# A hybrid decoder block on one core: memory attention by rounded parts, and elementwise work moved between VectorE and GpSimd

## The chip, the cores and the metric

The kernel runs on one core of a Trainium2 chip. The metric is the device time of one execution in microseconds (us). The engines are named as the profile names them: PE (TensorE matmuls), PEld (its weight loads), DVE (VectorE), ACT (ScalarE), POOL (GpSimd) and SP (SyncE, which here only issues DMAs). L12 is line 12 of the kernel before.

## The reference

One layer of a block with three mixers on 1024 tokens of width 1024, all in float32. Cut to what matters here:

```python
def hybrid_layer(x, mem, ...):
    h = rmsnorm(x, norm_g)
    proj = h @ w_in               # 1024 x 11280: the inputs of all branches and gates
    ...                           # gated DeltaNet branch, stick-breaking attention branch
    mkv = rmsnorm(mem, mem_norm_g) @ w_mem_kv      # 256 memory tokens
    mk, mv = jnp.split(mkv, 2, axis=-1)
    o_m = memory_attention(to_heads(m_q, 4), to_heads(mk, 4), to_heads(mv, 4))
    o_m = merge_heads(o_m) * jax.nn.silu(m_z)
    merged = g_dn * (o_dn @ w_br_dn) + g_sb * (o_sb @ w_br_sb) + g_m * (o_m @ w_br_mem)
    return x + merged @ w_out     # then a final rmsnorm

def memory_attention(q, mk, mv):  # 4 heads of 64
    s = jnp.einsum('bhtd,bhmd->bhtm', q, mk) * (1.0 / math.sqrt(q.shape[-1]))
    p = jax.nn.softmax(s, axis=-1)
    return jnp.einsum('bhtm,bhmd->bhtd', p, mv)
```

## The kernel before

**Products by rounded parts.** Most matmuls use the type fp32r. An operand is split into a high part (ACT copies it to fp32r) and a low part (DVE subtracts the high part from the source); `split` at L139 does both, and `mm3` at L153 multiplies as high x high + high x low + low x high. Products that stay in plain F32, the memory attention's among them, take a single call.

**The norm stage** (about the first 80 us). Rows of x are loaded 128 at a time into four buffers. `norm` (L270) squares on ACT, computes rs = 1/sqrt on POOL, and multiplies by the gain and rs: on DVE in one fused operation for the first two rows and the memory rows, or, with `on=gp`, as a product with the gain on POOL (L280) and a scaling on ACT (L284) for the other six rows of x. `two_rows` (L331) takes rows tb and tb+4, transposes them on PE, splits them into blocks A11, A12, A21, A22 and forms the sums S1 to S4 for a block scheme of Strassen and Winograd's kind, which saves one of eight block products in the large projection. The low parts of S1 to S4 are DVE subtracts of two SBUF tiles; those of the blocks read PSUM. Two row blocks at a time, `first_values` computes some values and the gates' inputs `bat`; its low part `svl` has one buffer, and POOL issues its store `sv_dl`. Beside this, `memory_kv` projects the memory tokens and stores mk and mv in DRAM (`kv_d`).

**The dense stream.** `stream` (L167) yields slots. One slot is one block product: 12 fp32r matmuls of 512 columns. A job has seven slots (B11, B21, T1, T2, T3, B22, T4) and four evacuations called `evac(i, j, a, b)`, the first of them, (0, 0), just before T2. Weights come over SP's queue into six buffers `wb`. All later stages call `slot()` between pieces of their own work, so the dense stream runs beside them.

**The decay tables.** After three slots the gate's chain on DVE (some 17 operations of 64 columns, ending in `gg`) feeds two small matmuls `gps` (L905), from which the tables come. They are stored and read back per head as `gam`; `decay` (L449) masks it on POOL and exponentiates it on ACT, at the first evacuation of each `kq_head`.

**The memory attention.** The job mq leaves q in SBUF (`mqT`), and `memory` (L659) is a generator whose steps are spread over 32 slots. Per head (64 channels) and per pair of token blocks: two score matmuls into a PSUM tile of the pair `wk`, the maximum on DVE, exponentials and scaling on ACT, four transposes on PE, a copy to `pT`. After four pairs come the values: two halves of two matmuls, a copy and a store. `combine` (the last part of the DeltaNet's triangular solve) uses the same two `wk` tiles in turn with it. The solver, a long chain on DVE, ends shortly after the memory attention starts.

**The order of the work.** The program is written in one order, and a scheduler orders each engine's instructions when the kernel is built. On the chip each engine and each DMA queue works through its list strictly in order. Tiles wait for the release of the buffer that they reuse.

Of the kernel before, what the change touches and what calls it, by code (L numbers as in the profile page):

```python
# [21 lines left out]
NT = 8  # L22
# [14 lines left out]
def hybrid_block(ctx, tc, x, mem, norm_g, mem_norm_g, wq, wv0, wba, convw, a_log, dt_bias,  # L37
# [51 lines left out]
    gp.memset(ones, 1.0)  # L89
    mhalf = cst.tile([P, 64], F32, name="mhalf")  # L90
    gp.memset(mhalf, -0.5)
# [31 lines left out]
    zm_d = dscr("zm_d", [2, P, T])  # L123
    kv_d = dscr("kv_d", [2, P, 2, 256])
    g_d = dscr("g_d", [3, 8, P, T])
# [12 lines left out]

    def split(dst, src):  # L139
        sc.activation(dst[0], src, AF.Copy)  # L140
        ve.tensor_tensor(out=dst[1], in0=src, in1=f(dst[0]), op=ALU.subtract)  # L141

# [117 lines left out]
    vp_ = pool("V0", 1, stack=v_st, side="right")  # L260
    bat = ap_.tile([P, NT, 16], F32, name="bat")

# [6 lines left out]

    def norm(xt, g_bc, nm, on=ve):  # L270

        sq = ap_.tile([P, T], mybir.dt.bfloat16, tag="sq", name="sq_" + nm)
        ss = ap_.tile([P, 1], F32, tag="ss", bufs=4, name="ss_" + nm)
        sc.activation(sq, xt, AF.Square, accum_out=ss)
        rs = ap_.tile([P, 1], F32, tag="rs", bufs=4, name="rs_" + nm)
        n = T // len(g_bc)
        halves = [(xt[:, j * n:j * n + n], g) for j, g in enumerate(g_bc)]
        if on is gp:
            for t, g in halves:
                gp.tensor_tensor(out=t, in0=t, in1=g, op=ALU.mult)  # L280
        gp.tensor_scalar(out=rs, in0=ss, scalar1=1.0 / T, scalar2=EPS, op0=ALU.mult, op1=ALU.add)
        gp.tensor_tensor(out=rs, in0=rs, in1=mhalf[:, 0:1], op=ALU.pow)
        if on is gp:
            sc.activation(xt, xt, AF.Copy, scale=rs)  # L284
        else:
            for t, g in halves:
                ve.scalar_tensor_tensor(out=t, in0=t, scalar=rs, in1=g, op0=ALU.mult, op1=ALU.mult)

    def transposed(xn, nm):
# [7 lines left out]
        return res  # L297

    def memory_kv():
        kv = [st.tile([P, 2, 256], F32, tag="st", bufs=3, name=f"kv{j}") for j in range(2)]  # L300
        for b in range(2):
            for q, ov in enumerate(transposed(mem_rows[b], f"m{b}")):
                split([t[:, q * 4:q * 4 + 4, b * P:b * P + P] for t in mHL], ov)
        for i in range(2):
            us = [unit(f"mk{i}_{j}", raw_unit(f"mk{i}_{j}", wmk[i, j])) for j in range(2)]
            o = psum("Y", f"mk_{i}")
            mm3(o[:, 0:256], [(us[k // 4][0][:, k % 4 * P:k % 4 * P + P], us[k // 4][1][:, k % 4 * P:k % 4 * P + P],
                               mHL[0][:, k, :], mHL[1][:, k, :]) for k in range(KC)])
            sc.activation(kv[0][:, i, :], o[:, 0:256], AF.Copy)
# [7 lines left out]
        sc.activation(kv[1], o.rearrange("p (a b) -> p a b", a=2), AF.Copy)  # L317
        for j in range(2):
            sc.dma_start(out=kv_d[j], in_=kv[j])

# [63 lines left out]
    for tb in range(1, 4):  # L384
        for b in (tb, tb + 4):
            if b not in rows_:
                rows_[b] = row(x, b)
            norm(rows_[b], [g1], f"x{b}", gp)
        two_rows(tb)()
# [53 lines left out]
    def kq_head(h):  # L443
# [68 lines left out]
        def evac(i, j, a, b):  # L512
            if (i, j) == (0, 0):
                decay()
            if j not in xps:
                xps[j] = xpad(cp, f"{'kq'[j]}{h}")
            put(xps[j][:, 4 + i * 512:516 + i * 512], a, b)
            if (i, j) == (0, 0):
                conv(0, 0)
            elif (i, j) == (0, 1):  # L520
                conv(1, 0)
                chunks(0)
                conv(1, 1)
            elif (i, j) == (1, 0):
                conv(0, 1)
                chunks(1)
                rows()
# [43 lines left out]
    def twice_silu(t, src, nm):  # L571

        th = mp_.tile([P, 512], F32, tag="th", bufs=2, name="th_" + nm)
        sc.activation(th, src, AF.Tanh, scale=0.5)
# [6 lines left out]

    mq = {}
# [76 lines left out]
    def memory():  # L659
        mkT, mv = (mp_.tile([P, 2, 256], F32, name=f"mkv{j}") for j in range(2))  # L660
        for j, t in enumerate((mkT, mv)):
            sy.dma_start(out=t, in_=kv_d[j])
        for h in range(4):
            r0 = (h % 2) * 64
            pT = mp_.tile([P, 2, T], F32, tag="pT", name=f"pT_{h}")
            for tb in range(0, NT, 2):
                s = psum("wk", f"ms_{h}_{tb}")
                for j in range(2):
                    pe.matmul(s[:, j * 256:(j + 1) * 256], mq[h // 2][r0:r0 + 64, (tb + j) * P:(tb + j + 1) * P],
                              mkT[r0:r0 + 64, h // 2, :], start=True, stop=True)  # L670
                sv = s.rearrange("p (a b) -> p a b", a=2)
# [15 lines left out]
                sc.activation(pT[:, :, tb * P:(tb + 2) * P], o.rearrange("p (a b) -> p a b", a=2), AF.Copy)  # L687
                yield
            for hf in range(2):
                mo = psum("wk", f"mo_{h}_{hf}")  # L690
                for c in range(2):
                    pe.matmul(mo[r0:r0 + 64, :], mv[:, c, h * 64:h * 64 + 64],
                              pT[:, c, half(hf)], start=(c == 0), stop=(c == 1))
                t = mp_.tile([P, 512], F32, tag="mot", bufs=1, name=f"mot_{h}_{hf}")
                sc.activation(t[r0:r0 + 64], mo[r0:r0 + 64], AF.Copy, scale=0.5)
                sc.dma_start(out=om_d[h // 2, r0:r0 + 64, half(hf)], in_=t[r0:r0 + 64])
            yield

# [103 lines left out]

    SOLVE, MEM, COMB, RECUR = 1 + 1 + 62 + 8, 4 * 5, 16, 1 + 16 * 4

# [56 lines left out]

    open_psum("psC", tr=2, wk=2, X=1)

    b_st = sub()
# [17 lines left out]

    aa, ab, ex, den, zz, z2, hr, sp, gg = (bt(n) for n in ("aa", "ab", "ex", "den", "zz", "z2", "hr", "sp", "gg"))
    ve.tensor_tensor(out=hn(aa), in0=bat[:, :, 8:16], in1=dtb.unsqueeze(1).to_broadcast([P, NT, H]), op=ALU.add)
# [8 lines left out]
    for c in (15, 13, 11, 9, 7, 5, 3):  # L893
# [5 lines left out]
                            op0=ALU.mult, op1=ALU.mult)  # L899
    for _ in range(3):  # L900
        slot()
# [19 lines left out]
    b_st.close()  # L921
    a_st.close()

    c_st = sub()
    cp = pool("C", 1, stack=c_st)
    until("kq7")
# [348 lines left out]
```

## Time and profile before

| | |
|---|---|
| median of 3 runs (lowest to highest) | 1628.33 us (1626.48 to 1635.07) |
| the profiled execution: time, span | 1628.7 us, 1627.0 us |
| its mean granted PE clock | 0.985 |
| busy share of the span: PE, PEld, DVE, ACT, POOL | 95%, 80%, 73%, 50%, 19% |
| DMA | 217.81 MB, mean 134 GB/s |

The span is the time from the first to the last instruction of the profiled execution. Busy shares are averages over the whole span; the stages differ, so the prediction reads them by stretches. "Idle before, releaser" in a row is the time for which the engine stood before the instruction, and what ended it.

### The profile page before, as it was taken

The numbers are of one execution on the slowest core, as the hardware profiler recorded it, in microseconds if no ns is written. First come the engines' busy times: TensorE is split into PE (matmuls) and PEld (weight loads), VectorE is DVE, ScalarE is ACT, GpSimd is POOL, SyncE is SP. The second block draws the span as 40 slices with busy tenths as digits, with TensorE's granted clock in tenths as the row PEclk, the third lists the DMA queues.
The fourth block names the chain that finished last, engine by engine and source line by source line (L and its number), as shares of the span: only waits on it lengthen the run. The fifth ranks groups of instructions, "written<-read, shape, count | busy, mean of one in ns | idle before, by whom it ended". The sixth has DMA issues, their size and how long they took to land.

```text
span 1627.0 us, 23179 instructions
## 1 busy us (share of the span) xinstructions
PE 1552.1 (95%) x7963; PEld 1294.8 (80%) x7963; DVE 1179.9 (73%) x1891; ACT 817.6 (50%) x1909; POOL 303.5 (19%) x557
## 2 busy tenths in 40 slices
PE   5889999999999999999999999999998899989998
PEld 4868888887888777776688888888886788878786
DVE  8869889888999998554588778777867554554333
ACT  7548778775555334555555555555544222232121
POOL 4314444351122110000011112111111111010011
PEclk8999999999999999999999999999998999999999
DMA  7236555564333445333222322332148765634232
GB/s 268 94 90 176 159 183 166 158 193 148 97 107 108 141 136 165 91 111 96 90 85 85 110 93 82 104 92 79 65 155 262 254 202 181 206 122 138 82 104 78
DMA packets 149063, 217.81 MB, mean 134 GB/s; under 512 B 39504, under 2 KB 66384, under 8 KB 148688
## 3 DMA queue, kind: packets, MB, share of 16 engines
q1 hardware_dynamic: 105824, 157.06, 32.2%
q10 hardware_dynamic: 34016, 29.89, 5.5%
q0 software_dynamic: 9104, 29.37, 4.8%
q8 instruction: 63, 1.03, 0.3%
q14 instruction: 56, 0.46, 0.1%
HBM read 147.48 MB, written 68.78 MB: 133 GB/s over the span
## 4 chain that ended last, share of the span: by engine, by line
PE 64%; DVE 4%; DMA 4%; issue 3%; ACT 1%; POOL 1%; SPq 0%; DVEq 0%; POOLq 0%; ACTq 0%
PE mmY_g L157 3%; PE mmY_g L159 3%; PE mmY_g L158 3%; PE mmY_skq L157 2%; PE aTp L1014 2%; PE mmY_skq L159 2%; PE mmY_skq L158 2%; PE out L1183 2%; PE out L1181 2%; PE out L1182 2%; PE y_ysb L1116 2%; PE y_ysb L1117 2%; PE y_ydn L1116 2%; PE y_ysb L1118 2%; PE y_ydn L1117 2%
## 5 line engine op out<-in xcount | busy, mean ns | idle before, releaser
L988 DVE TENSOR_TENSOR_SCAN pf<-pf 128x512 f32<-128x512 f32 (+4 forms) x96 | 97.2, 1013 | 16.4 <-POOL pf L986 16.4
L140 ACT ACTIVATE aTh<-aTp 128x512 fp32r<-128x512 f32 (+2 forms) x96 | 44.7, 498 | 62.2 <-PE aTp L1014 58.6
L973 POOL MEMSET pf<- 128x1 f32 x64 | 6.0, 98 | 342.7 <-PE aTp L1014 175.4
L141 DVE TENSOR_TENSOR aTl<-aTp,aTh 128x512 fp32r<-128x512 f32 (+2 forms) x96 | 50.4, 547 | 22.8 <-ACT aTh L140 22.6
L982 ACT ACTIVATE pf<-z 128x512 f32<-128x512 f32 (+4 forms) x96 | 47.1, 498 | 26.7 <-PE z L159 23.4
L986 POOL TENSOR_SCALAR_AFFINE_SELECT pf<-pf 128x128 f32<-128x128 f32 x64 | 24.9, 390 | 181.4 <-ACT pf L982 181.4
L991 DVE TENSOR_TENSOR pf<-be,pf 128x512 f32<-128x512 f32 (+4 forms) x96 | 53.7, 559 | 3.9
L647 DVE TENSOR_TENSOR M<-M,tmp 128x62 f32<-128x62 f32 (+30 forms) x62 | 53.6, 864 | 0.3
L644 DVE TENSOR_TENSOR tmp<-M 128x62 f32<-128x62 f32 (+30 forms) x62 | 53.3, 860 | 0.3
L1116 PE MATMUL y_ysb<-oh_sb,w_ysb 128*128 128x512 f32 x128 | 51.0, 399 | 2.0 <-ACT w_ysb L140 2.0
L1181 PE MATMUL out<-oh_wo,mh 128*128 128x512 f32 x128 | 50.0, 391 | 1.5 <-ACT mh L140 1.5
L1116 PE MATMUL y_ydn<-odnh,w_ydn 128*128 128x512 f32 x128 | 49.5, 391 | 1.8 <-ACT odnh L140 1.8
L1117 PE MATMUL y_ysb<-ol_sb,w_ysb 128*128 128x512 f32 x128 | 50.8, 397 | 0.0
L1118 PE MATMUL y_ysb<-oh_sb,w_ysb 128*128 128x512 f32 x128 | 50.8, 398 | 0.0
L1030 PE MATMUL av<-aTl,vh 128*128 128x256 f32 (+1 forms) x160 | 46.9, 293 | 3.4 <-DVE aTl L141 3.4
L1117 PE MATMUL y_ydn<-odnl,w_ydn 128*128 128x512 f32 x128 | 49.9, 390 | 0.0
L1118 PE MATMUL y_ydn<-odnh,w_ydn 128*128 128x512 f32 x128 | 49.9, 390 | 0.0
L1182 PE MATMUL out<-ol_wo,mh 128*128 128x512 f32 x128 | 49.8, 389 | 0.0
L983 ACT ACTIVATE be<-z 128x512 f32<-128x512 f32 (+4 forms) x96 | 47.4, 503 | 4.2 <-DVE pf L991 4.2
L1183 PE MATMUL out<-oh_wo,ml 128*128 128x512 f32 x128 | 49.3, 389 | 0.0
L1029 PE MATMUL av<-aTh,vh 128*128 128x256 f32 (+1 forms) x160 | 45.1, 282 | 1.3 <-ACT aTh L140 1.3
L1188 DVE TENSOR_TENSOR xo<-out,xo 128x512 f32<-128x512 f32 x16 | 11.1, 692 | 48.0 <-PE out L1183 48.0
(803 smaller groups left out, 5513.8 us busy)
## 6 DMA issues: line engine op xcount, KB each, us to landing
wb_g_b<-in_wq_dram SPq DMA_DIRECT2D x48, 256.0 KB, 3.0
wb_kq_b<-in_wq_dram SPq DMA_DIRECT2D x32, 256.0 KB, 2.8
wb_skq_b<-in_wq_dram SPq DMA_DIRECT2D x32, 256.0 KB, 2.6
g_d<-g ACTq DMA_DIRECT2D x32, 256.0 KB, 2.0
xt<-in_x_dram SPq DMA_DIRECT2D x8, 512.0 KB, 4.3
wb_sz_b<-in_wq_dram SPq DMA_DIRECT2D x16, 256.0 KB, 3.3
gam<-gr_d SPq DMA_DIRECT2D x8, 512.0 KB, 4.2
er<-er_d SPq DMA_DIRECT2D x16, 256.0 KB, 3.8
```

What stands on the lines that cost most here:

```text
L157: pe.matmul(o, ah, bh, start=(first and i == 0), stop=False, **kw)
L158: pe.matmul(o, ah, bl, start=False, stop=False, **kw)
L159: pe.matmul(o, al, bh, start=False, stop=(i == n - 1), **kw)
L647: ve.tensor_tensor(out=d, in0=d, in1=t, op=ALU.add)
L988: ve.tensor_tensor_scan(out=pv[:, ::-1], data0=pv[:, ::-1], data1=pv[:, ::-1], initial=pf[:, off + c1:off + c1 + 1], op0=ALU.mult, op1=ALU ...
L991: ve.tensor_tensor(out=d, in0=be, in1=d, op=ALU.mult)
L1116: pe.matmul(oo[hf], wh, oh[:, s], start=(k == 0), stop=False)
L1117: pe.matmul(oo[hf], wh, ol[:, s], start=False, stop=False)
L1118: pe.matmul(oo[hf], wl, oh[:, s], start=False, stop=(k == n - 1))
L1181: pe.matmul(oo[hf], mh[:, k, :], wo[k][0][:, s], start=(k == 0), stop=False)
L1182: pe.matmul(oo[hf], mh[:, k, :], wo[k][1][:, s], start=False, stop=False)
L1183: pe.matmul(oo[hf], ml[:, k, :], wo[k][0][:, s], start=False, stop=(k == KC - 1))
```

## The change

- Memory attention: mk and mv (`memory_kv`) and q (`mq_evac`) are split into high and low parts and stored in DRAM (`mk_d`, `mv_d`, `mqs_d`). Per head, q's high part is loaded into partitions 0 to 63 and its low part into 64 to 127, and k's high part into both halves, so one matmul with a contraction of 128 gives q_high k_high + q_low k_high; a second of 64 adds q_high k_low. The weights are split too, and the values are computed with `mm3`. Values are taken after each half, so a head has six steps and not five.
- Low parts of S1 to S4 are subtracted on POOL (`split(..., gp)`).
- All norms use the fused product on DVE.
- Before the decay tables four slots run and not three. For that `bat` moves to the constant pool, and pool A is closed and pool C opened earlier; head 0's `decay` is called at its evacuation (1, 1).
- Small ones: `th` has one buffer and not two, the tables of the gate chain share tiles, `mhalf` is narrower.

```diff
-    def split(dst, src):
+    def split(dst, src, on=ve):
         sc.activation(dst[0], src, AF.Copy)
-        ve.tensor_tensor(out=dst[1], in0=src, in1=f(dst[0]), op=ALU.subtract)
+        on.tensor_tensor(out=dst[1], in0=src, in1=f(dst[0]), op=ALU.subtract)
...
-    def norm(xt, g_bc, nm, on=ve):
+    def norm(xt, g_bc, nm):
...
-        if on is gp:
-            for t, g in halves:
-                gp.tensor_tensor(out=t, in0=t, in1=g, op=ALU.mult)
         gp.tensor_scalar(out=rs, in0=ss, scalar1=1.0 / T, scalar2=EPS, op0=ALU.mult, op1=ALU.add)
         gp.tensor_tensor(out=rs, in0=rs, in1=mhalf[:, 0:1], op=ALU.pow)
-        if on is gp:
-            sc.activation(xt, xt, AF.Copy, scale=rs)
-        else:
-            for t, g in halves:
-                ve.scalar_tensor_tensor(out=t, in0=t, scalar=rs, in1=g, op0=ALU.mult, op1=ALU.mult)
+        n = T // len(g_bc)
+        for j, g in enumerate(g_bc):
+            t = xt[:, j * n:j * n + n]
+            ve.scalar_tensor_tensor(out=t, in0=t, scalar=rs, in1=g, op0=ALU.mult, op1=ALU.mult)
...
+    def stored_split(d, src, nm, q):
+
+        t = [st.tile([P, 512], F32, tag="st", bufs=3, name=f"{nm}{j}") for j in "hl"]
+        r = [v.rearrange("p (a b) -> p a b", a=2) for v in t] if len(src.shape) == 3 else t
+        split([v.bitcast(F32R) for v in r], src)
+        for v, o in zip(r, d):
+            q.dma_start(out=o, in_=v)
...
         def sums(*names):
             for n in names:
-                split(tuple(t[:, :, ts] for t in hb[n]), ss_[n])
+                split(tuple(t[:, :, ts] for t in hb[n]), ss_[n], gp)
...
         def evac(i, j, a, b):
-            if (i, j) == (0, 0):
+            if (i, j) == (0, 0) and h > 0 or (i, j) == (1, 1) and h == 0:
                 decay()
...
     def mq_evac(i, j, a, b):
-        if j not in mq:
-            mq[j] = mp_.tile([P, T], F32, name=f"mqT{j}")
-        put(mq[j][:, half(i)], a, b)
+        if b is not None:
+            t = staged(f"mq_{i}{j}")
+            put(t, a, b)
+            a = t
+        stored_split([mqs_d[k, 2 * j:2 * j + 2, :, half(i)].rearrange("h r t -> (h r) t") for k in range(2)],
+                     a, f"mq{i}{j}", sc)
...
         for h in range(4):
-            r0 = (h % 2) * 64
-            pT = mp_.tile([P, 2, T], F32, tag="pT", name=f"pT_{h}")
+            i, r0 = h // 2, (h % 2) * 64
+
+            q = mp_.tile([P, T], F32R, tag="q", bufs=2, name=f"q_{h}")
+            k = mp_.tile([P, 2, 256], F32R, tag="k", bufs=2, name=f"k_{h}")
+            for j in range(2):
+                sy.dma_start(out=f(q[j * 64:j * 64 + 64]), in_=mqs_d[j, h])
+                sy.dma_start(out=f(k[j * 64:j * 64 + 64, 0, :]), in_=mk_d[0, i, r0:r0 + 64])
+            sy.dma_start(out=f(k[0:64, 1, :]), in_=mk_d[1, i, r0:r0 + 64])
             for tb in range(0, NT, 2):
...
                 for j in range(2):
-                    pe.matmul(s[:, j * 256:(j + 1) * 256], mq[h // 2][r0:r0 + 64, (tb + j) * P:(tb + j + 1) * P],
-                              mkT[r0:r0 + 64, h // 2, :], start=True, stop=True)
+                    ts = slice((tb + j) * P, (tb + j) * P + P)
+                    pe.matmul(s[:, j * 256:(j + 1) * 256], q[:, ts], k[:, 0, :], start=True, stop=False)
+                    pe.matmul(s[:, j * 256:(j + 1) * 256], q[0:64, ts], k[0:64, 1, :], start=False, stop=True)
...
-                sc.activation(pT[:, :, tb * P:(tb + 2) * P], o.rearrange("p (a b) -> p a b", a=2), AF.Copy)
+                split([t[:, :, c0:c0 + 256] for t in pT], o.rearrange("p (a b) -> p a b", a=2))
                 yield
-            for hf in range(2):
+                if c0 == 0:
+                    continue
+                hf = tb // 4
                 mo = psum("wk", f"mo_{h}_{hf}")
-                for c in range(2):
-                    pe.matmul(mo[r0:r0 + 64, :], mv[:, c, h * 64:h * 64 + 64],
-                              pT[:, c, half(hf)], start=(c == 0), stop=(c == 1))
-                t = mp_.tile([P, 512], F32, tag="mot", bufs=1, name=f"mot_{h}_{hf}")
+                hs = slice(i * P, i * P + P)
+                mm3(mo, [(mv[0][:, c, hs], mv[1][:, c, hs], pT[0][:, c, :], pT[1][:, c, :])
+                                        for c in range(2)])
+                t = staged(f"mot_{h}_{hf}")
...
-    SOLVE, MEM, COMB, RECUR = 1 + 1 + 62 + 8, 4 * 5, 16, 1 + 16 * 4
+    SOLVE, MEM, COMB, RECUR = 1 + 1 + 62 + 8, 4 * 6, 16, 1 + 16 * 4
...
-    for _ in range(3):
+    for _ in range(4):
         slot()
```

More of the change, by code (lines that the diff above doesn't have):

```diff
@@ L89, in hybrid_block @@
     gp.memset(ones, 1.0)
-    mhalf = cst.tile([P, 64], F32, name="mhalf")
+    mhalf = cst.tile([P, 8], F32, name="mhalf")
     gp.memset(mhalf, -0.5)
@@ L260, in hybrid_block @@
     vp_ = pool("V0", 1, stack=v_st, side="right")
-    bat = ap_.tile([P, NT, 16], F32, name="bat")
+    bat = cst.tile([P, NT, 16], F32, name="bat")
     mHL = [t.rearrange("p a b -> p (a b)").rearrange("p (k t) -> p k t", k=KC) for t in hb["S4"]]
@@ L303, in memory_kv @@
                 split([t[:, q * 4:q * 4 + 4, b * P:b * P + P] for t in mHL], ov)
+        o = psum("Y", "mk")
         for i in range(2):
             us = [unit(f"mk{i}_{j}", raw_unit(f"mk{i}_{j}", wmk[i, j])) for j in range(2)]
[L306 to L309, printed above, removed]
+            mm3(o[:, i * 256:i * 256 + 256],
+                [(us[k // 4][0][:, k % 4 * P:k % 4 * P + P], us[k // 4][1][:, k % 4 * P:k % 4 * P + P],
+                  mHL[0][:, k, :], mHL[1][:, k, :]) for k in range(KC)])
+        stored_split([d.rearrange("i p t -> p i t") for d in (mk_d[0], mk_d[1])], o.rearrange("p (a b) -> p a b", a=2), "mk", sc)
         us = [unit(f"mv_{j}", raw_unit(f"mv_{j}", wmv[j])) for j in range(4)]
@@ L316, in memory_kv @@
                   us[k // 2][1][:, k % 2 * 256:k % 2 * 256 + 256]) for k in range(KC)])
-        sc.activation(kv[1], o.rearrange("p (a b) -> p a b", a=2), AF.Copy)
-        for j in range(2):
-            sc.dma_start(out=kv_d[j], in_=kv[j])
+        stored_split([mv_d[j] for j in range(2)], o.rearrange("p (a b) -> p a b", a=2), "mv", sc)
     def first_values(b, blocks):
@@ L387, in hybrid_block @@
                 rows_[b] = row(x, b)
-            norm(rows_[b], [g1], f"x{b}", gp)
+            norm(rows_[b], [g1], f"x{b}")
         two_rows(tb)()
@@ L571, in twice_silu @@
     def twice_silu(t, src, nm):
-        th = mp_.tile([P, 512], F32, tag="th", bufs=2, name="th_" + nm)
+        th = mp_.tile([P, 512], F32, tag="th", bufs=1, name="th_" + nm)
         sc.activation(th, src, AF.Tanh, scale=0.5)
@@ L862, in hybrid_block @@
     open_psum("psC", tr=2, wk=2, X=1)
+    a_st.close()
+    c_st = sub()
+    cp = pool("C", 1, stack=c_st)
     b_st = sub()
@@ L921, in hybrid_block @@
     b_st.close()
-    a_st.close()
-    c_st = sub()
-    cp = pool("C", 1, stack=c_st)
     until("kq7")
```

24 lines of the change are left out of this document (13 added, 11 removed).

## The prediction

> **What bounds the kernel now.** I read the page first, then the busy time by stretch, then the rows of single instructions at the edited places. Below are the page's span and first row, then rows of the stretches (stretch, its length, busy us of PE, PEld, DVE, ACT, POOL with counts, granted clock, DMA share, GB/s).
>
> ```profile
> span 1627.0 us, 23179 instructions
> PE 1552.1 (95%) x7963; PEld 1294.8 (80%) x7963; DVE 1179.9 (73%) x1891; ACT 817.6 (50%) x1909; POOL 303.5 (19%) x557
> ...
> 20.00:52.00 32.00, 22.09 (x158) 20.45 (x156) 29.36 (x33) 22.00 (x40) 23.62 (x20) 0.84 0.57 180
> 81.00:95.00 14.00, 9.01 (x38) 6.86 (x37) 9.07 (x28) 4.00 (x10) 3.11 (x7) 0.89 0.26 66
> 590.00:640.00 50.00, 43.90 (x180) 34.16 (x179) 44.73 (x76) 20.31 (x41) 3.11 (x5) 0.93 0.43 137
> 640.00:760.00 120.00, 120.00 (x625) 87.56 (x624) 62.05 (x111) 61.22 (x137) 0.00 (x0) 1.00 0.37 110
> 800.00:1200.00 400.00, 398.10 (x2124) 342.47 (x2123) 315.66 (x492) 219.43 (x457) 62.42 (x168) 1.00 0.29 92
> ```
>
> PE bounds the whole, but not each stage. In the norm stage (20 to 52) DVE is busy 29 of 32 us and PE 22; from 81 to 95 no engine is full; from 590 to 640, the solver's end, DVE is as full as PE; from 640 PE is full and DVE and ACT are half empty. A microsecond of PE work is worth a microsecond only from 640 on. What the front saves is handed on: the later stages start earlier.
>
> **A. The memory products (640 to 800).** The two F32 score matmuls of a tile (contraction 64, 256 columns) become four fp32r ones; the two F32 value matmuls (512 columns) become six fp32r ones.
>
> ```profile
> 682.92 0.39 PE L157 MATMUL mmZ_dz<-hS4h,wu_dz_B 128*128 128x512 f32 x1
> 683.15 0.39 PE L158 MATMUL mmZ_dz<-hS4l,wu_dz_B 128*128 128x512 f32 x1
> 683.47 1.13 PE L669 MATMUL ms<-mkv,mqT 64*128 64x256 f32 x4
> 684.52 0.50 PE L159 MATMUL mmZ_dz<-hS4h,wu_dz_B 128*128 128x512 f32 x1
> 684.86 0.40 PE L157 MATMUL mmZ_dz<-hS4h,wu_dz_B 128*128 128x512 f32 x1
> ...
> 709.58 0.39 PE L157 MATMUL mmX_mz<-hA12h,wu_mz_B 128*128 128x512 f32 x1
> 709.89 1.93 PE L692 MATMUL mo<-pT,mkv 128*64 128x512 f32 x4
> 711.75 0.50 PE L158 MATMUL mmX_mz<-hA12l,wu_mz_B 128*128 128x512 f32 x1
> ...
> 38.92 0.28 PE L159 MATMUL mk<-hS4h,wu_mk 128*128 128x256 f32 x1
> 39.04 0.28 PE L157 MATMUL mk<-hS4h,wu_mk 128*128 128x256 f32 x1
> ```
>
> Matmuls overlap, so I price by starts, not durations. fp32r of 512 columns: 683.15 - 682.92 = 0.23; of 256 columns: 0.12. A score pair holds PE from 683.15 + 0.23 to 684.52, 1.14, and the start after that comes 0.34 on instead of 0.23: 1.25 a tile. 16 tiles: 20.0 against 16 x 4 x 0.12 = 7.7; saved 12.3. A value tile: 711.75 - 709.81 = 1.94, with the same slow re-entry 2.05; 8 tiles: 16.4 against 8 x 6 x 0.23 = 11.0; saved 5.4. Together 17.7 of PE work.
>
> How much of it shortens the run? First all waits of PE from 640 to 800, then rows that bear on the start of the stage.
>
> ```profile
> PE mmY_g L157 <- DVE mz L575: 1.4, 1, 1.4
> PE mo L692 <- ACT pT L687: 0.7, 1, 0.7
> ...
> 607.55 1.99 PE L669 MATMUL ms<-mkv,mqT 64*128 64x256 f32 x8
> 652.64 1.13 PE L669 MATMUL ms<-mkv,mqT 64*128 64x256 f32 x4
> 626.05 0.60 ACT L242 ACTIVATE mqT<-mmY_mq 128x512 f32<-128x512 f32 x1 [0.38 <-PE mmY_mq L159]
> 614.97 14.59 SPq L150 DMA_DIRECT2D wb_dz_b<-in_wq_dram  x4
> DMA to landing us min/median/max: 3.6/3.9/4.2
> ```
>
> PE waits 2.1 in 160, so work taken away there counts, except two of the 16 score tiles (607.55) that lay in the DVE-bound stretch: 1.5 less. q now goes through DRAM, so the first scores need all of the first pair's q: 626.65, then a store and a load of about 3.9 (the landing of mkv, the last row). That is after 633 instead of 607, and costs nothing, since the third score tile runs only at 652 today. New on DVE are 16 low parts of the weights (0.68 each, 10.9), in a stretch where it has 58 of 120 free. Late next: the chain transposes, high, low, values is 0.7 longer, and each head's five loads of q and k stand in SP's in-order queue, where four weight loads that wait for buffers took 14.59. Ends: -17.7 (all counts) and 0 (waits replace it). PE's 2.1 of waiting is nearest to the first: I take **-14**.
>
> **B. q's evacuation** adds a rounding on ACT (0.6) and a low part on DVE (0.68) for four pieces, before the solver ends, and takes three store buffers a piece of the three there are. DVE is busy 44.73 of 50 there, so of its 4 x 0.68 = 2.7 I let little hide: **+2** (0 to +6, a stall per piece). th with one buffer and the low parts of mk and mv fall on engines with room, priced in C or 0.
>
> **C. The norm stage.**
>
> ```profile
> 42.40 2.74 POOL L280 TENSOR_TENSOR xt<-xt,g 128x1024 f32<-128x1024 f32 x1
> 43.39 0.67 DVE L141 TENSOR_TENSOR hA22l<-xT_x,hA22h 128x512 fp32r<-128x512 f32 x1
> 43.99 1.70 DVE L141 TENSOR_TENSOR wu_kq_B<-wb_kq_b,wu_kq_B 128x512 fp32r<-128x512 f32 x1
> ...
> L280 POOL TENSOR_TENSOR xt<-xt,g 128x1024 f32<-128x1024 f32 x6 | 14.8, 2472 | 3.9 <-ACT sq_x L274 3.8
> L141 DVE TENSOR_TENSOR wu_kq_B<-wb_kq_b,wu_kq_B 128x512 fp32r<-128x512 f32 x5 | 5.9, 1190 | 4.0 <-ACT wu_kq_B L140 4.0
> L141 DVE TENSOR_TENSOR hS2l<-S,hS2h 128x512 fp32r<-128x512 f32 x4 | 5.7, 1420 | 0.0
> L141 DVE TENSOR_TENSOR wu_mv<-wb_mv,wu_mv 128x512 fp32r<-128x512 f32 x4 | 5.5, 1400 | 0.0
> L141 DVE TENSOR_TENSOR wu_mk<-wb_mk,wu_mk 128x512 fp32r<-128x512 f32 x4 | 4.7, 1197 | 0.0
> L141 DVE TENSOR_TENSOR hS3l<-S,hS3h 128x512 fp32r<-128x512 f32 x4 | 2.7, 680 | 0.0
> L287 DVE SCALAR_TENSOR_TENSOR xt<-xt,rs_x,g 128x1024 f32<-128x1024 f32 x2 | 2.5, 1281 | 0.4 <-DMA g<-in_norm_g_dram 0.4
> ...
> 73.24 0.42 DVE L141 TENSOR_TENSOR svl<-v,svh 128x256 fp32r<-128x256 f32 x1 [1.85 <-DMA sv_dl<-svl]
> ```
>
> hA22l, which reads one input from PSUM, ran beside POOL's product in 0.67. The next subtract, with both inputs in SBUF, started at 43.99 and ended at 45.69, just after POOL's 45.14. So POOL's products lock out DVE's two-SBUF operations. The same instruction takes 680 ns where nothing locks it (hS3l); the excess of the four groups above it is 5 x 0.51 + 4 x 0.74 + 4 x 0.72 + 4 x 0.52 = 10.5.
>
> Removed: six products on POOL (14.8), the 10.5 of lock, 16 low parts on DVE (16 x 0.68 = 10.9), six scalings on ACT. Added: six fused products on DVE (6 x 1.28 = 7.7), low parts of mk and mv (1.4), and 16 subtracts on POOL of half the width of the 2.47, so an estimated 1.25 each, 20 in all. They lock DVE too, but its neighbours are then mostly reads of PSUM; if half of that hits, 10. DVE's sum: -10.5 - 10.9 + 7.7 + 1.4 + 10 = -2, and -12 without overlap. Each row's path is also shorter by POOL's product less DVE's (2.47 - 1.28). Against it: POOL issues sv_dl's store in order, now behind these subtracts, and the next svl waits for the landing (73.24). Ends: -12, and +25 (12 of 1.25 on that store chain, and 20 - 10.5 more lock). DVE, not that chain, fills the stage, which is nearer to the first: **-5**.
>
> GPSIMD Engine Reference in the Trainium skill, section 3.1, speaks against this part: it gives a two-input add of 2048 elements as 1.96 times as long on GpSimd as on VectorE and keeps VectorE as the rule for elementwise work. Its section 1 says that GpSimd's SBUF interfaces are shared with VectorE, with contention for instructions of two SBUF inputs; the rows at 43.39 and 43.99 agree. By that rule part C loses, which is the third rival.
>
> **D. The gap before the decay tables (87 to 101).**
>
> ```profile
> 91.83 0.57 PE L905 MATMUL gps<-gg,tri 128*128 128x64 f32 x2 [3.94 <-DVE gg L898]
> 94.58 0.80 PE L157 MATMUL mmX_kq<-hA12h,wu_kq_B 128*128 128x512 f32 x1 [0.72 <-ACT xp_k L244]
> 95.17 0.63 PE L158 MATMUL mmX_kq<-hA12l,wu_kq_B 128*128 128x512 f32 x1
> 95.60 0.63 PE L159 MATMUL mmX_kq<-hA12h,wu_kq_B 128*128 128x512 f32 x1
> 101.14 2.45 ACT L455 ACTIVATE gam<-gam,tab_nG 128x128 f32<-128x128 f32 x8 [5.14 <-POOL gam L452]
> ```
>
> Three dense slots go ahead of the gate's chain; PE then waits 3.94 for gg. A fourth slot (12 x 0.23 = 2.7) now stands before it, and its evacuation frees the PSUM tile that costs 0.72 at 94.58. After the wait matmuls start 0.43 apart instead of 0.23 for about ten: up to 2 more if the idle time goes. Head 0's decay moves later, so ACT's 5.14 behind gam no longer holds k's convolution; gam itself comes no sooner. Ends: -7 and 0 (the slot only delays gps); the 2.7 that is certain to be there, and some clock: **-4**.
>
> **The sum.** The profiled execution took 1628.7 (span 1627.0), 0.4 above the median of the runs, 1628.33. -14 + 2 - 5 - 4 = -21, so **1607 us**, -1.3%.
>
> **Rivals.**
> 1. *The memory saving is hidden.* Scores, values and the combine products share two PSUM buffers in a fixed order; if their chain and not PE sets the stage's end, the 14 becomes PE idle time. For it: a value product waited 0.7 for pT. Against: PE busy 120.00 of 120.00. 1628.7 + 2 - 5 - 4 = 1622: no measurable change.
> 2. *The loads of q and k come late (slower).* If heads 1 to 3 find q behind weight loads held like those at 614.97, each loses 14.6 less the two dense slots that cover it, about 10: 1628.7 + 30 - 21 = 1638. From 7 a head on (21 / 3) it eats the whole gain. Against: two buffers for q let a load go a head early.
> 3. *POOL becomes the norm stage's bound*, with 13 of the 25 above: 1628.7 - 14 + 2 + 13 - 4 = 1626, no measurable change.
>
> **Chances.** Forecast 0.64; rival 1 0.16; rival 2 0.12; rival 3 0.08. Half a per cent, 8 us, is what a measurement here tells from no change: below 1620 is faster, above 1636.5 slower. Faster 0.70 (the forecast, and 0.06 of rival 1 where part of the 14 comes through), same 0.18, slower 0.12. The forecast's own range is 1595 to 1620; with rivals 1 and 3 and the ends of A to D it is 1592 to 1630.
>
> **What would show it.** A: PE's busy time in the memory stage falls by some 17, with starts 0.12 and 0.23 apart and still no waits. B: waits of ACT or DVE on the stores of q. C: no DVE row of 2 to 3 us beside POOL, and a shorter way to the first dense matmul. D: the 3.94 is under 1.5. It is wrong if PE stands after 640, if scores wait for q's load, or if svl waits longer for sv_dl.

## The result: slower by 0.8%, and two rows that say where

| | before | after |
|---|---|---|
| median of 6 runs each (lowest to highest) | 1631.63 us (1626.48 to 1635.07) | 1643.98 us (1642.20 to 1647.38) |
| ratio, 95% interval | | 1.0079 [1.0056, 1.0102] |
| span of the profiled execution | 1627.0 us | 1643.0 us |
| first dense product; first product of dz; first product of the stage behind the memory stage (z) | 76.8; 591.6; 802.3 | 67.7; 578.6; 824.3 |

The forecast was 1607, range 1592 to 1630. The front saved 13 us (first dz 591.6 to 578.6), more than the 9 forecast. The memory stage, from the first dz to the first z, grew from 210.7 to 245.7 us, 35 where 12 were to be saved. Some 8 of these 35 are work that only changed its place: 2590 dense products stand ahead of the first z in the kernel after and 2556 before it, and 34 at 0.23 are 7.8; behind the first z the kernel after is 6.0 us shorter. One run of e15 below was far slower than its others (2214.5 us at a granted clock of 0.654); it counts in the median given for e15 and not in its ratio. The page of the kernel after, and its stretches in the order of the prediction's (stretch, length, busy us of PE, PEld, DVE, ACT, POOL with counts, granted clock, DMA share, GB/s):

```profile
span 1643.0 us, 23267 instructions
PE 1552.3 (94%) x7979; PEld 1301.8 (79%) x7979; DVE 1181.6 (72%) x1903; ACT 820.3 (50%) x1909; POOL 315.2 (19%) x567
...
20.00:52.00 32.00, 26.32 (x184) 24.48 (x183) 32.00 (x45) 22.59 (x43) 19.94 (x20) 0.87 0.64 208
81.00:95.00 14.00, 14.00 (x63) 11.62 (x62) 12.97 (x32) 7.25 (x13) 1.73 (x1) 1.00 0.27 76
590.00:640.00 50.00, 24.60 (x99) 17.82 (x97) 34.47 (x61) 14.27 (x29) 0.88 (x1) 0.77 0.53 162
640.00:760.00 120.00, 115.09 (x622) 88.14 (x623) 62.03 (x114) 60.75 (x141) 0.00 (x0) 0.97 0.39 107
578.60:824.30 245.70, 212.54 (x1057) 163.30 (x1056) 141.97 (x246) 111.07 (x238) 3.24 (x7) 0.92 0.41 121
```

From 81 to 95 PE no longer stands (9.01 before, 14.00 now). From 590 to 640 it works 24.60 of 50 us, where it worked 43.90. PE's and ACT's rows around that hole, and the end of the solver on DVE, all of the kernel after (start, length, engine, line, operation, idle time before and what ended it):

```profile
614.49 0.39 PE L161 MATMUL mmY_dz<-hS3h,wu_dz_T 128*128 128x512 f32 x1
619.24 2.15 PE L699 MATMUL mT<-ident,pt 128*128 128x128 f32 x8 [4.36 <-ACT pt L695]
642.45 1.94 PE L725 MATMUL Y<-tmpc 64*64 64x64 f32 x16 [21.06 <-DMA tmpc<-mo_d]
644.32 0.79 PE L159 MATMUL mo<-pTh,mvh 128*128 128x512 f32 x1
644.91 0.63 PE L160 MATMUL mo<-pTl,mvh 128*128 128x512 f32 x1
645.34 0.63 PE L161 MATMUL mo<-pTh,mvl 128*128 128x512 f32 x1
...
647.28 0.59 ACT L711 ACTIVATE mot<-mo 64x512 f32<-64x512 f32 x1 [25.26 <-PE mo L161]
647.77 0.58 ACT L246 ACTIVATE dz<-mmZ_dz 128x512 f32<-128x512 f32 x1
...
624.84 0.27 DVE L650 TENSOR_TENSOR M<-M,tmp 128x62 f32<-128x62 f32 x1
```

PE stands 21.06 us for the combine's first product, Y, whose data come from the solver (X is its second product). The solver's last step is at 624.84. Its result still has to be copied, stored and loaded: the last copy on DVE, at 634.16, waits 7.06 for the store of an earlier one, and SP issues the loads from 638.21 on. In the kernel before, Y runs 21.9 us behind the last step (629.7 to 651.6) and PE does not wait for it, since dense products run meanwhile. Nothing dense fills the hole: the dense evacuation at 647.77 runs on ACT right behind mot, the copy of the first memory product, which waited 25.26. In TensorE's instruction list of the kernel after, 2100 dense products stand ahead of the first Y; before it were 2174. And the scores, priced at starts 0.12 apart:

```profile
668.03 0.39 PE L160 MATMUL mo<-pTl,mvh 128*128 128x512 f32 x1
668.26 0.40 PE L161 MATMUL mo<-pTh,mvl 128*128 128x512 f32 x1
668.49 0.28 PE L682 MATMUL ms<-k,q 128*128 128x256 f32 x1
668.70 0.38 PE L683 MATMUL ms<-k,q 64*128 64x256 f32 x1
669.01 0.38 PE L682 MATMUL ms<-k,q 128*128 128x256 f32 x1
669.32 0.38 PE L683 MATMUL ms<-k,q 64*128 64x256 f32 x1
```

The values start 0.23 apart, as forecast. The scores, which alternate between a contraction of 128 and of 64 rows, start 0.31 apart: 4 x 0.31 = 1.24 a tile, against 1.25 before. That saving is nil.

### The profile page after: what moved, and what is told of

It reads as the page before. It is cut to its first block, busy times and chain, and to the rows that moved or that the text cites. A ratio compares the mean times of both kernels' runs of the same rounds, so it can differ in the third digit from the quotient of the medians.

```text
span 1643.0 us, 23267 instructions
## 1 busy us (share of the span) xinstructions
PE 1552.3 (94%) x7979; PEld 1301.8 (79%) x7979; DVE 1181.6 (72%) x1903; ACT 820.3 (50%) x1909; POOL 315.2 (19%) x567
## 4 chain that ended last, share of the span: by engine, by line
PE 71%; DVE 8%; DMA 8%; issue 8%; ACT 3%; POOL 2%; SPq 0%; DVEq 0%; ACTq 0%; POOLq 0%
PE mmY_g L159 2%; PE mmY_g L161 2%; PE mmY_g L160 2%; PE out L1200 2%; PE out L1198 2%; PE out L1199 2%; PE y_ysb L1133 2%; PE mmY_skq L159 2%; PE y_ysb L1134 2%; PE y_ydn L1133 2%; PE y_ysb L1135 2%; PE y_ydn L1135 2%; PE y_ydn L1134 2%; PE aTp L1031 2%; PE mmY_skq L161 2%
## 5 line engine op out<-in xcount | busy, mean ns | idle before, releaser
L647 DVE TENSOR_TENSOR tmp<-M 128x62 f32<-128x62 f32 (+30 forms) x62 | 53.2, 859 | 0.2
L1048 PE MATMUL av<-aTh,vl 128*128 128x256 f32 (+1 forms) x160 | 46.3, 289 | 0.0
```

The costliest lines, as they stand in the source:

```text
L647: ve.tensor_tensor(out=t, in0=M[:, 0:j, j].unsqueeze(2).to_broadcast([P, j, b]), in1=M[:, j, j + 1:64].unsqueeze(1).to_broadcast([P, j, b] ...
```

## The experiments

**The hole: buffers or something else.** Theory: `mot` took a place in the three `st` buffers in turn with the dense evacuations, and its product waits in the two `wk` tiles behind Y. Four kernels on one chip:

```diff
# e1: the kernel after, mot out of st
-                t = staged(f"mot_{h}_{hf}")
+                t = mp_.tile([P, 512], F32, tag="pt", bufs=2, name=f"mot_{h}_{hf}")
# e2: the kernel after, scores with one contraction
-            sy.dma_start(out=f(k[0:64, 1, :]), in_=mk_d[1, i, r0:r0 + 64])
+            for j in range(2):
+                sy.dma_start(out=f(k[j * 64:j * 64 + 64, 1, :]), in_=mk_d[1, i, r0:r0 + 64])
...
-   pe.matmul(s[:, j * 256:(j + 1) * 256], q[0:64, ts], k[0:64, 1, :], start=False, stop=True)
+   pe.matmul(s[:, j * 256:(j + 1) * 256], q[:, ts], k[:, 1, :], start=False, stop=True)
# e3: both.  e4: the kernel after, combine later
-        if pos[0] - first > SF * total:
+        if pos[0] - first > SF * total + 2:
```

> The changed kernel with one line other: mot, the copy of a memory product on its way to DRAM, takes a buffer of memory's own pt rotation instead of one of the three st buffers that the dense stream's evacuations use. Theory (buffers): the 21.06 us stand of TensorE at Y comes from mot_0_0 holding its place in the st rotation: it waits for mo_0_0, which stands behind Y_0 in the two wk tiles, so the dense evacuations behind mot cannot go on and the order of TensorE has no dense product between the last mT and Y_0. With mot apart, the order of TensorE holds 120 more dense products ahead of Y_0 (2220 against 2100), 120 x 0.24 = 29 us of work: the stand goes from 21 us to under 3, and the time from 1644 to 1618-1625. Rival (th with one buffer, or the q parts' stores, throttle the dense stream): the stand stays at 15 us or more and the time at 1638-1646.

> The changed kernel with the second score product at the full contraction: k's low part is loaded twice (rows 0 to 63 and 64 to 127) and multiplied with the whole stacked q, so the four products of a score tile all have shape 128x128 by 128x256. Theory (alternation): the spacing of 0.31 us of a score product comes from alternating contractions of 128 and 64; with one shape it falls to about 0.12, a tile from 1.24 to 0.5 us, and TensorE's work by 16 x 0.75 = 12 us; the stand at Y stays near 21 us, so the time falls by 4-12 us, to 1632-1640. Rival (every new 256-column product costs 0.31 because of its weights): the spacing stays at 0.25 or more and the time at 1642-1647.

> Both edits: mot in the pt rotation and the score products at one contraction. If both theories hold the two gains add, 20-25 and 8-12 us: 1608-1616. If the alternation theory falls it stands with the mot edit alone, 1618-1625; if both fall, at 1640-1647.

> The changed kernel with mot still in the st rotation, but the combine starting two slots later, so that mo_0_0 is written ahead of Y_0 in the wk rotation. Theory (buffers): mot_0_0 no longer waits behind Y_0; 48 more dense products stand ahead of Y_0 in TensorE's order (2148 against 2100), 11.5 us: the stand falls from 21 us to 6-12 us and the time to 1628-1636. Rival (the loads of the combine, or th and the q parts, set the stand): Y_0 waits as long as before, 18 us or more, and the time stays at 1640-1647.

| | median us | ratio to before, 95% interval | PE's wait at Y | stage, first dz to first z | PE busy in it | of it at a clock of 0.50 |
|---|---|---|---|---|---|---|
| before | 1629.1 | | 0.0 | 210.7 | 201.9 | 6.8 |
| after | 1644.0 | 1.0079 [1.0056, 1.0102] | 21.1 | 245.7 | 212.5 | 14.3 |
| e1 | 1636.3 | 1.0028 [1.0014, 1.0043] | 6.0 | 228.6 | 206.0 | 21.7 |
| e2 | 1629.8 | 0.9991 [0.9977, 1.0006] | 20.7 | 232.9 | 200.1 | 10.7 |
| e3 | 1625.1 | 0.9970 [0.9953, 0.9987] | 6.2 | 221.9 | 200.0 | 32.2 |
| e4 | 1638.6 | 1.0057 [1.0042, 1.0072] | 6.5 | 244.2 | 222.7 | 37.0 |

The row after is from the result, where before took 1631.6; times from different chips are compared by their ratios. The stages of after, e2 and e4 hold the 34 dense products more. e1, e3 and e4 came out above the forecast of their theories, e2 just below it. Stages and waits are those of one profiled execution each.

PE's longest waits in the memory stage of the kernel after, and then of e1 with both of its waits at Y (waited for, sum, times, longest):

```profile
PE Y L725 <- DMA tmpc<-mo_d: 21.1, 1, 21.1
PE mT L699 <- ACT pt L695: 4.4, 1, 4.4
```

```profile
PE mT L699 <- ACT pt L695: 4.2, 2, 2.3
PE Y L725 <- DMA tmpc<-mo_d: 3.7, 2, 2.2
...
PE Y L725 <- ACT pt L691: 2.3, 1, 2.3
```

The hole goes with the buffer: in e1, whose program differs in nothing but the place of `mot`, 2220 dense products stand ahead of Y and the longest wait is 2.3. The `th` buffer and q's stores, unchanged in e1, did not make it. e4 agrees: with mot still in `st`, but its product ahead of Y in the `wk` tiles, the wait at Y falls to 6.5. But e1 gained 8 us and not 20: the dense stream then runs ahead and is used up early, and the last three heads' X have no dense product between them. The last 43.5 us of the stage in e3 and, for comparison, in the kernel with the change's front alone (e5, below):

```profile
757.00:800.50 43.50, 31.18 (x164) 0.73 0.30 79
```

```profile
745.30:788.80 43.50, 40.08 (x209) 0.96 0.28 71
```

There PE stands 12.3 us between the last heads' small products, against 3.4, and its mean granted clock is 0.73 against 0.96. At a clock of 0.50 products start 0.43 apart and not 0.23 (last section), so about half of PE's busy time at 0.50 is lost. Time taken out of the hole came back in part at the stage's end, as stands and as lost clock. In e4 the time fell by 4 to 5 us (its interval and that of after overlap), though the wait at Y fell by 15: PE counts 10 us more of busy time in the stage. The clock accounts for that: 37.0 us of it are at 0.50, against 14.3, and half of the difference is 11. The same stretch of e4, and then of the kernel after:

```profile
644.30:664.80 20.50, 17.16 (x88) 0.50 0.38 95
```

```profile
644.30:664.80 20.50, 20.50 (x103) 0.92 0.46 119
```

The contraction is the clear case, here four rows of e2:

```profile
663.06 0.28 PE L683 MATMUL ms<-k,q 128*128 128x256 f32 x1
663.17 0.28 PE L684 MATMUL ms<-k,q 128*128 128x256 f32 x1
663.29 0.28 PE L683 MATMUL ms<-k,q 128*128 128x256 f32 x1
663.41 0.28 PE L684 MATMUL ms<-k,q 128*128 128x256 f32 x1
```

With one shape they start 0.12 apart, although the weights change at every second one. PE's busy time over the run falls from 1552.3 to 1541.9, and the time by 14 us, though the stand at Y stays at 20.7. So of the two repairs the shape of the scores is worth more time than the buffer, 14 us against 8.

**The two halves of the change, each alone.**

```diff
# e5: before + norm, lows, pools, four slots, decay call (all of the front); memory attention as before
# e6: before + memory attention, stores and th; of the front only the pools (as in e9)
```

> The kernel before with the change's front alone: the norm's products on VectorE, the lows of S1 to S4 on GpSimd, four dense slots ahead of the decay tables, the first decay call moved, the small tables' aliases; memory attention as before. Theory (front carries): the dense stream starts near 67.7 us instead of 76.8 and kk near 101 instead of 119; the order of TensorE in the memory stage is that of before (2174 dense products ahead of the first Y), so the 13-14.5 us of the front reach the end: 1613-1619. Rival (the solver's end holds the stage: after the change Y_0 came only 9 us earlier though dense came 13 us earlier): 1620-1625.

> The kernel before with the change's memory attention alone (parts stored and loaded, stacked scores, values in three products, mot in the st rotation); the front as before, but for where bat and two pools lie. Theory (the order is at fault): TensorE's order has 2100 dense products ahead of Y_0 as in the changed kernel, the stand at Y is 15-25 us whatever the front does, and the time is 1650-1660. Rival (the faster front itself made the stand, by bringing the dense stream ahead of the solver's result): with the old front the stand at Y is under 10 us and the time 1635-1645.

e5 took 1615.7 us, 0.9918 [0.9903, 0.9933]; first dz at 576.2, first z at 788.8, the stage 212.6 long: the front's gain reaches the end. e6 took 1646.3, 1.0110 [1.0091, 1.0128], with the whole hole under the old norm, lows and slots (its first dz is at 582.6):

```profile
PE Y L731 <- DMA tmpc<-mo_d: 21.0, 1, 21.0
```

So neither these parts of the front nor the pools made the hole: e5 has them all, and no wait at Y. e6's time fell below the expectation of 1650 to 1660; the pools, which it had to take along for room, are worth some 10 us by themselves (next).

**Which part of the front.**

```diff
# e7: the kernel after, lows of S1 to S4 back on DVE
-                split(tuple(t[:, :, ts] for t in hb[n]), ss_[n], gp)
+                split(tuple(t[:, :, ts] for t in hb[n]), ss_[n])
# e8: the kernel after, norm's products back on POOL (norm(..., gp) for x's rows)
# e9: before, with this moved (and, for room, bat and the small tables as in after)
     open_psum("psC", tr=2, wk=2, X=1)
+    a_st.close()
+    c_st = sub()
+    cp = pool("C", 1, stack=c_st)
...
     b_st.close()
-    a_st.close()
-
-    c_st = sub()
-    cp = pool("C", 1, stack=c_st)
# e15: e5 without the lows on POOL
```

> The changed kernel with the low parts of S1 to S4 back on VectorE; one look at the front, the time is secondary. Theory (VectorE bound the norm stage, and the 16 lows of 1.4 us on GpSimd relieved it): the dense stream starts at 71-77 us instead of 67.7. Rival (the norm's products alone brought the gain): it starts at 66-69 us.

> The changed kernel with the norm's products back on GpSimd (and the scaling on ScalarE) while the lows stay there too; one look at the front. Theory (GpSimd in the chain of each row was what bound the norm stage): the dense stream starts at 76 us or later, as before the change or worse since GpSimd has 22 us of lows besides. Rival (the lows are the gain, the norm's place is indifferent): it starts at 66-70 us.

> The kernel before with one thing of the change: the C pool, which takes the evacuations of the first kq jobs, is opened ahead of the decay tables' pool (with bat among the constants, and the small tables sharing buffers, which makes the room); norm, lows, the number of slots, the decay call and the memory attention as before. Theory (the pool's place is the larger part of the front's gain): the dense stream starts at 75-77 us as before, but kk comes at 106-109 us instead of 119 and the first dz at 582-584 instead of 591.6; time 1618-1622 beside 1629. Rival (the gain needs the faster norm): kk at 115 us or later and time 1626-1630.

> The change's front alone with the lows of S1 to S4 left on VectorE: memory attention and lows as before, the norm's products, the pools, four slots and the decay call as changed. Theory (the lows on GpSimd are worth nothing: in the changed kernel taking them back moved the first dz by -1.0 us): 1613-1618, the same as the front alone at 1615.7. Rival (they are worth the 2 us at the dense start): 1617-1620.

The first dense product and the first one of dz: after; e7; e8; e9 (before: 76.84 and 591.63).

```profile
67.66 0.39 PE L159 MATMUL mmZ_kq<-hS1h,wu_kq_T 128*128 128x512 f32 x1
578.56 0.47 PE L159 MATMUL mmY_dz<-hA11h,wu_dz_B 128*128 128x512 f32 x1
```

```profile
69.67 0.39 PE L159 MATMUL mmZ_kq<-hS1h,wu_kq_T 128*128 128x512 f32 x1
577.57 0.47 PE L159 MATMUL mmY_dz<-hA11h,wu_dz_B 128*128 128x512 f32 x1
```

```profile
75.30 0.49 PE L159 MATMUL mmZ_kq<-hS1h,wu_kq_T 128*128 128x512 f32 x1
582.84 0.47 PE L159 MATMUL mmY_dz<-hA11h,wu_dz_B 128*128 128x512 f32 x1
```

```profile
76.45 0.40 PE L157 MATMUL mmZ_kq<-hS1h,wu_kq_T 128*128 128x512 f32 x1
581.08 0.47 PE L157 MATMUL mmY_dz<-hA11h,wu_dz_B 128*128 128x512 f32 x1
```

e9 starts its dense stream no earlier than before and reaches dz 10.5 us earlier; it took 1620.9 us, 0.9940 [0.9917, 0.9964]. PE is busy all 60.0 us from 76 to 136 there, against 53.2 before. So most of the front's 13 us is the earlier pool, which takes the first evacuations while the tables are made. For the rest, e7 and e8 are one execution each, and the nine kernels here that have the whole change's front scatter: they start the dense stream at 66.3 to 67.7 and dz at 575.8 to 578.6. Norms on POOL again (e8) cost 7.6 us at the dense start and 4.3 at dz, clear of that. The lows back on DVE (e7) cost 2 us at the dense start and nothing that can be told at dz; e15 starts its dense stream at 67.93, like e5, and took 1614.3, 0.9892 [0.9858, 0.9927], no measurable difference from e5. These two have the lowest medians of all.

**What e3 still loses against the front alone (9 us).** A new theory was the solver: its last step starts at 625.3 in e3 and 624.8 in the kernel after, against 614.5 in e5, since DVE, busy 36.0 of the 38.4 us from the first dz to the end of that step in the kernel before, has 42.8 to do there in the kernel after (q's low parts, pT's, more dense work). The edit issues the solver and the combine earlier; SF is the share of the stage's dense slots over which the solver is spread.

```diff
-SF = 0.72
+SF = 0.66
```

> The changed kernel with SF 0.66 instead of 0.72, and nothing else: the solver's 72 steps are spread over 79 dense slots instead of 86, so its last step and the combine's first are issued seven slots earlier; TensorE's order still has 2100 dense products ahead of the first Y. Theory (the stand at Y lasts as long as the solver on VectorE is late): the solver's last step moves from 625 us to 608-617 us, the stand at Y falls from 21 us to under 12, and the time from 1644 to 1628-1637. Rival (the stand comes from buffers alone, whenever the solver ends): the stand stays over 15 us and the time at 1640-1647.

> The kernel with mot in the pt rotation and full-contraction scores, with SF 0.66. Theory (what is left of its loss is the solver's end: last step at 625.5 us against 614.8 with the old memory attention, which leaves two heads of the combine without dense work beside them): the solver ends at 608-617 us, Y_0 comes at 628-637 instead of 645, the stands in the stage's last 45 us fall from 12 us to under 6, time 1612-1619 instead of 1625. Rival (the tail is the memory attention's own chain of two wk tiles): the tail keeps its 10 us or more and the time stays at 1622-1627.

> The change's front alone, memory attention as before, with SF 0.66: a try for a better version, and a control on the SF edit. There TensorE has no stand at Y to take away (0.0 us), so by the theory of the solver's end the edit is worth little: 1612-1617 beside 1615.7. If SF itself were worth 8 us or more whatever the memory attention, it would fall to 1608 or less.

| | median us | ratio, 95% interval | solver's last step | wait at Y |
|---|---|---|---|---|
| e10 (after) | 1651.0 | 1.0124 [1.0098, 1.0150] | 619.0 | 28.0 |
| e11 (e3) | 1629.1 | 0.9985 [0.9970, 1.0000] | 619.9 | 0.5 |
| e12 (e5) | 1625.8 | 0.9961 [0.9947, 0.9975] | 611.1 | 4.1 |

The theory fell. The solver ended 3 to 6 us sooner, and no kernel became faster: e12 is slower than e5, e10 slower than after at the edge of the intervals, and e11 cannot be told from e3. All three lie above every range that was given for them. In e12 the stage is 219.4 us long, 6.8 longer than in e5, and 4.9 of that are busy time of PE; the clock accounts for these, for 12.8 us of the busy time are at 0.50, against 3.4. e10 shows more of the buffer's part: now Y, X and the next Y stand ahead of the first mo in PE's list, still with 2100 dense products ahead of all, and the waits grow to

```profile
PE Y L725 <- DMA tmpc<-mo_d: 28.0, 3, 22.4
```

This fits the buffer's theory: the hole lasts for whatever stands between mot and the end of its wait, not for the solver's lateness alone. The last theory was the tail: with other paces the last heads of the combine lie beside dense products again.

```diff
# e13: e3 with                       e14: the same, 24.0
-        mem_((pos[0] - start2) / 32.0)
+        mem_((pos[0] - start2) / 28.0)
...
-            comb((pos[0] - first - SF * total) / ((0.98 - SF) * total))
+            comb((pos[0] - first - SF * total) / ((0.86 - SF) * total))
```

> The kernel with mot in the pt rotation and full-contraction scores, with the memory's steps spread over 28 slots instead of 32 and the combine's to 0.86 of the stage instead of 0.98. In TensorE's order the sixth, seventh and eighth head's X then stand behind 2472, 2520 and 2544 dense products instead of 2544 each (front alone: 2471, 2508, 2544). Theory (the 10 us that this kernel still loses against the front alone are stands in the tail of the stage, where the last heads of the combine and the memory have no dense product between them, because the dense stream ran ahead while Y_0 waited for the solver): the stands in the last 45 us fall from 12 to 4-8 us and the time from 1625 to 1616-1621. Rival (the new memory attention costs 10 us more wherever it stands, in ScalarE and VectorE work): the time stays at 1623-1628.

> The same with the memory's steps over 24 slots: the sixth to eighth X stand behind 2472, 2544 and 2544 dense products, and the memory's last four value tiles behind 2531 and 2544. Same theory: in between the two, 1618-1624; rival: 1623-1628.

e13 took 1618.3 us, 0.9915 [0.9892, 0.9938], the time expected; e14 1625.7, 0.9973 [0.9953, 0.9993], the rival's. The last 43.5 us of e13's stage:

```profile
747.30:790.80 43.50, 33.22 (x137) 0.65 0.22 67
```

The stands there fell to 10.3, not to 4 to 8: the combine now ends 39 us earlier, and the memory's heads are alone. Its stage is 214.7 us long, against 221.9 in e3 and 212.6 in e5: 7 of the 9 us lay in the order of the work and not in a cost that the new attention has wherever it stands. Since e14, with a faster pace of the memory, did not follow, which order gives the rest stays open.

With these repairs the new memory attention ties with the old one (0.9915 against 0.9918 and 0.9892), though it has less work for PE. Half of the busy time at a clock of 0.50 taken off, PE's work in the stage is an estimated 184 us in e3 and in e13 (198.8 busy, 28.7 of them at 0.50) and 199 in e5 (200.6, 3.4). These 15 us go into stands, 15.9 in e13 against 12.0, and above all into lost clock, 14 against 2. Nearly all of e13's slow time is one stretch of the tail:

```profile
757.40:788.10 30.70, 21.82 (x61) 0.50 0.16 46
```

No run tried to keep the clock up there, so whether the new attention would then win is open.

## Why the prediction was wrong, step by step

- **A, the price of a score tile** (-12.3): the 0.12 came from products of equal shape (mk). The list alternates contractions, and there a product costs 0.31. Measured: 1.24 a tile, saving 0, and 0.12 as soon as the shapes agree (e2), which is worth 14 us of time. The values' price (0.23) held, and with the shapes repaired so did most of the 17.7 of PE work: an estimated 15 (e3 and e13 beside e5).
- **A, "late next" and the choice of -14**: this step failed most. I asked whether PE waits in the stage of before and found 2.1 us, and then kept the order of before, so the worst end that I allowed was 0. I named the chain of transposes (PE's waits for it rose from 0.7 to 2.9) and the loads of q (no wait of PE for them), and passed over one line of the diff, `mot` from a buffer of its own into `st`. That ties the dense evacuations to a product behind Y: 21 us of hole, the largest wait, priced at nothing. Taken away alone it gave back 8 us (e1), since the filler was then missing at the stage's end. Clock lost behind stands and in the tail was priced nowhere in A.
- **B, q's evacuation** (+2): the four low parts of 0.68 on DVE are there, and PE waits 1.1 us for one of them. The solver's last step moved from 38.1 us behind the first dz (629.7 - 591.6) to 46.2 (624.8 - 578.6). e10 to e12, where the solver ends sooner and no time is won, speak against its passing into the time one for one.
- **C and D** (-5 and -4): right in sign, 13 us together where 9 were forecast, and divided wrongly. D, the pools and the gap before the tables, gave about 10. PE's wait for gg, 3.94, is gone, as D asked, but it is gone in e9 too, with three slots: the pool did it, and not the fourth slot by which D was priced. C is left with 2 to 4, from the norm's products: e8 loses 4.3 at dz, and e5 gains 2.4 more than e9 (their intervals overlap, and e5 has the fourth slot too). The lows on POOL were a wash.
- **Rivals.** The first came nearest: the order in the two `wk` tiles does make the memory's saving into idle time, but its price stopped at a saving of nothing. The second, late loads of q, did not occur: the first is issued at 602.4, and the first scores run at 609.4, not after 633 as A had it. In the third the rows are these, POOL's and DVE's groups of the kernel after from 0 to 100 us, and then DVE's of e7:

```profile
L143 POOL TENSOR_TENSOR hS2l<-S,hS2h 128x512 fp32r<-128x512 f32 x4 | 5.6, 1391 | 1.9 <-ACT hS2h L142 1.9
...
L283 DVE SCALAR_TENSOR_TENSOR xt<-xt,rs_x,g 128x1024 f32<-128x1024 f32 x8 | 11.5, 1449 | 0.7 <-DMA g<-in_norm_g_dram 0.7
```

```profile
L283 DVE SCALAR_TENSOR_TENSOR xt<-xt,rs_x,g 128x1024 f32<-128x1024 f32 x8 | 10.1, 1277 | 0.6 <-DMA g<-in_norm_g_dram 0.6
L143 DVE TENSOR_TENSOR hS2l<-S,hS2h 128x512 fp32r<-128x512 f32 x4 | 2.7, 680 | 0.0
```

A low part takes 1391 ns on POOL and 680 on DVE, 2.0 times, and DVE's products beside it 1449 instead of 1277. The 1.96 of the Trainium skill (GPSIMD Engine Reference, section 3.1, for an add of 2048 elements) agrees. The rule that the prediction takes from there was right in that the lows gained nothing on POOL; the loss feared in the rival did not come either: POOL is busy 19.94 of the 32 us from 20 to 52.

## What to carry to other kernels

Before pricing a change by an engine's idle time, go through every buffer that moves into a shared rotation and ask what its slowest user waits for: everything allocated behind it then waits too, and a build-time order may be rebuilt around that wait. Price matmuls from rows with the same sequence of shapes, not only the same shape. And when a hole is closed, look at the end of the stage: if the filler was only moved forward, the hole is there. Read PE's busy time beside its granted clock: a repair that takes waiting away can give it back as slow work.

## What the runs showed of the hardware

An fp32r product of 256 columns starts 0.12 us after its neighbour among products of equal contraction, and 0.31 after it where contractions of 128 and 64 rows alternate, though the smaller one does half the work. The weight loads (PEld) show where the time goes. Here are two of the kernel after, whose products start at 668.70 and 669.01, and two of e2, whose products start at 663.17 and 663.29:

```profile
668.70 0.18 PEld L683 LDWEIGHTS ms<-k,q 64*128 64x128 f32 x1 [0.25 <-issue]
669.01 0.19 PEld L682 LDWEIGHTS ms<-k,q 128*128 128x128 f32 x1
```

```profile
663.06 0.19 PEld L684 LDWEIGHTS ms<-k,q 128*128 128x128 f32 x1
663.18 0.19 PEld L683 LDWEIGHTS ms<-k,q 128*128 128x128 f32 x1
```

With equal shapes the load starts 0.11 ahead of its product, under the product before; with alternating ones it starts only with its own product. That speaks for the mixture, and not the 64 rows, as the cause: the plain F32 scores of the kernel before, all of 64 rows, load ahead too (a load at 683.79 for the product at 684.00). The TensorE page of the Trainium skill (TensorE: Matmul & The Clock Gate, section "Why this matters for your kernels") says that a single product with a small contraction takes the same time as a full one; no run here has fp32r products of 64 rows alone, and the mixture took two and a half times as long.

The stand also costs clock behind it. The rows of the kernel after around the hole (stretch, length, PE busy, granted clock, DMA share, GB/s):

```profile
614.90:617.00 2.10, 0.00 (x0) 1.00 0.20 78
617.10:619.20 2.10, 0.00 (x0) 0.50 0.00 0
621.40:642.40 21.00, 0.00 (x0) 0.50 0.50 156
642.45:647.70 5.25, 5.25 (x27) 0.50 0.00 0
647.80:650.00 2.20, 2.20 (x18) 1.00 0.27 60
```

The clock fell in the stand before the hole, some 2.2 us after PE's last product had ended at 614.88, and the 2.15 us of transposes between the two stands did not bring it back. Behind the hole PE runs at 0.50 for 5.3 us more: the values that follow start 0.43 apart and not 0.23 (645.34 after 644.91). The same page (Part 1) lets the clock fall to half after an idle window of about 3.4 us and return after about as long a busy one; measured are 2.2 and 5.3. The whole stretch at 0.50, from 617.05 to 647.77, lasts 30.72 us, nine times the 3.41 of the only one in e5's memory stage (from 751.47).
